# Mixers of a streaming-encoder layer: where the first weights, the state-space input and the projections' weights come from

## The chip, the cores and the metric

The kernel runs on one core of one Trainium2 chip. The metric is the device time of one execution in microseconds, the median of several. TensorE (PE) multiplies matrices, VectorE (DVE) and ScalarE (ACT) work on elements, GpSimd (POOL) gathers rows, and SyncE (SP) issues most transfers; ACT and POOL issue transfers too. Each engine runs its own instructions in order and waits on semaphores for the others.

## The reference

One layer over 1024 tokens of width 1024, float32: two token mixers in parallel on one input projection, then a retrieval of experts.

```python
xn = rms_norm(h, norm1_g)
p = xn @ w_in                                  # 1024 x 1536
xa, gate, us = p[..., :512], p[..., 512:1024], p[..., 1024:]
ya = rg_lru_group(xa, gate, ...)               # conv, gates, linear scan, times gelu(gate)
yb = s5_group(us, ...)                         # complex state-space scan, gelu, gated unit
y = concat([rms_norm(ya, gnorm_lru), rms_norm(yb, gnorm_s5)])
h = h + y @ w_out
h = h + peer_ffn(rms_norm(h, norm2_g), ...)    # 8 heads, top 16 of 128 x 128 experts
out = rms_norm(h, normf_g)
```

## The kernel before

**Precision.** Each large product is made of three: both operands are split into a high part (ACT copies it to the type fp32r) and a low part (DVE subtracts), and PE adds high x low, low x high and high x high. So every weight costs a transfer, an ACT copy and a DVE subtraction before PE can use it.

**Stages.** `front` (from L150) computes the mixers, up to the output projection and the second norm. `peer` (from L948) computes the queries, picks experts for all tokens, gathers rows for three blocks of 128 tokens (POOL fetches them, DVE consumes them) and treats the other five blocks densely: a first part that works ahead and stores its rows to DRAM (`aa` to `A_d`), and a steady part, `dense`, whose order is written out by hand.

**How the order comes about.** In `front` and in the first part of `peer` the pieces are Python generators. `Merge.run` keeps a planned clock for each engine, charges every instruction a planned cost, and lets the generator with the smallest clock plus bias emit next. A generator can wait for a flag by yielding its name. The framework then schedules the emitted instructions once more by its own cost model, with the emitted order as priority, so an instruction can be moved ahead of others that are not ready. Buffers are rings: a tile with `tag` and `bufs=n` waits until the tile n before it has been read for the last time.

**PSUM.** All eight banks are shared out in `front`: `pt` has four, `pj` two, `pu` two (L158 to L160).

**The first product, `us_first` (L258).** It computes columns 1024 to 1279 of the input projection, the first half of the state-space input, for eight groups of 128 tokens at once, in all eight banks (`held`), with a loop over eight slices k of the contraction. Each slice needs `split_x(k)` (L207) and a split slice of the weights (`wgroup`, L231). The weights `w0` come in one transfer of 1 MB from ACT's queue (L229), while SP's queue brings eight slices of x of 512 KB (L195). Beside it run `squares` (L213: the sums of squares of x, then `rc`, the reciprocal root per token, and its broadcast `rstdb` through PE, named spr) and `setup` (the state-space coefficients). When all slices are done, `us_first` waits for the flag "rc", and ACT copies each bank into `Vt` scaled by `rc` (`us_out`, L255).

**The rest of the input projection.** `proj(grp, ...)` (L604) computes 256 columns: it first has `wgroup` load and split eight weight slices of 128 x 256 (raw tiles `wr` with two buffers, split tiles `wh` and `wl` with nine), then makes four PSUM tiles, two halves e of 128 columns by two halves i of the tokens, 24 matmuls each, and DVE evacuates each with `rstdb`. `us_second` (L277) does columns 1280 to 1535. `proj_thread` (L685) runs proj 0, `us_second`, proj 1, and then proj 2 and 3 (the gates) after the flags "ut1" and "ut3", since their outputs take the place of `Vt`.

**Their consumers.** `quarter(q)` (L434) is the state-space scan for a quarter of the groups, mostly DVE; it starts its transposes of `Vt` (utp) after "us0" or "us1", and SP moves its matrix T in eight transfers (L479). `lru(m)` (L628) is the other mixer, for each 128 columns of proj 0 and 1. `glu` (L724, PSUM tiles glp) is the gated unit, `norm` (L784) gives the scales `rg`.

**Output projection, `w_out` (L813).** Sixteen PSUM tiles (`wop`) for each half, twelve matmuls each; DVE adds each to `h`, scaled by `rg` of that half. Both halves take `pj`, that is two banks.

Of the kernel before, what the change touches and what calls it, by code (L numbers as in the profile page):

```python
# [7 lines left out]
F32 = mybir.dt.float32  # L8
F32R = mybir.dt.float32r
# [3 lines left out]
AF = mybir.ActivationFunctionType  # L13
ALU = mybir.AluOpType
# [4 lines left out]
P = 128  # L19
D = 1024  # L20
T = 1024
L = 8
# [127 lines left out]
def front(tc, a, cst, nd, mg):  # L150


    nc = tc.nc
    V, S, G, PE = mg.V, mg.S, mg.G, mg.PE
# [3 lines left out]
    pt = lambda n: ps.tile([P, 512], F32, tag="mm", name=n, bufs=4)  # L158
    pj = lambda n: ps.tile([P, 512], F32, tag="pj", name=n, bufs=2)
    pu = lambda n: ps.tile([P, 512], F32, tag="us", name=n, bufs=2)  # L160
    keep = pools.open("fkeep")
    pxa = pools.open("fxa", "right")
    xa = [pxa.tile([P, 3 + T], F32, name=f"xa{m}") for m in range(4)]
# [3 lines left out]
    rstdb = keep.tile([P, T], F32, name="rstdb")  # L167
    rc = keep.tile([P, L], F32, name="rc")
# [5 lines left out]
    xh = pin.tile([P, 8, T], F32R, name="xh")  # L174
    xl = pin.tile([P, 8, T], F32R, name="xl")
# [7 lines left out]
    def t(shape, name):  # L183
        return pset.tile([P] + shape, F32, name=name)
# [5 lines left out]
    S.dma_start(Cin, a["s5c"])  # L190
    px = pools.open("fx")
    xrs = []
    for k in range(8):
        xr = px.tile([P, T], F32, name="xr", tag="xr", bufs=8)
        nc.sync.dma_start(xr, a["xT"][k * P:(k + 1) * P, :])  # L195
        xrs.append(xr)

    def spread(col):

# [7 lines left out]
    def split_x(k):  # L207
        S.activation(xh[:, k, :], xrs[k], AF.Copy, scale=g1[:, k:k + 1])
        V.scalar_tensor_tensor(xl[:, k, :], xrs[k], g1[:, k:k + 1], xh[:, k, :].bitcast(F32),
                               ALU.mult, ALU.subtract)  # L210
# [15 lines left out]
    pw = pools.open("fw", "right", bufs=9)  # L226
    pq = pools.open("fq", "right")
    w0 = pq.tile([P, 8, 256], F32, name="w0")
    nc.scalar.dma_start(w0, a["w_in"][:, 1024:1280].rearrange("(k p) n -> p k n", p=P))  # L229

    def wgroup(col, width, out, whole=None):  # L231

        for k in range(8):
            if whole is None:
                r = pw.tile([P, width], F32, tag="wr", name="wr", bufs=2)
                nc.sync.dma_start(r, a["w_in"][k * P:(k + 1) * P, col:col + width])
            else:
                r = whole[:, k]
            h = pw.tile([P, width], F32R, tag="wh", name="wh")
            lo = pw.tile([P, width], F32R, tag="wl", name="wl")  # L240
            S.activation(h, r, AF.Copy)
            V.tensor_tensor(lo, r, h.bitcast(F32), ALU.subtract)
            out.append((h, lo))
            yield


    Vt = {}

    def us_product(o, s, k, w):
        sl = slice(s * P, s * P + P)  # L250
        PE.matmul(o, xh[:, k, sl], w[k][1], start=(k == 0), stop=False)
        PE.matmul(o, xl[:, k, sl], w[k][0], start=False, stop=False)
        PE.matmul(o, xh[:, k, sl], w[k][0], start=False, stop=(k == 7))

    def us_out(hf, s, pp):  # L255
        S.activation(Vt[hf][:, :, s, :], pp.rearrange("p (g i) -> p g i", i=16), AF.Copy, scale=rc[:, s:s + 1])

    def us_first():  # L258

        w, held = [], [(pu if s < 2 else pj if s < 4 else pt)("usp")[:, :256] for s in range(L)]  # L260
        ws = wgroup(1024, 256, w, w0)
        for k in range(8):
            split_x(k)
            next(ws)
            yield
            for s in range(L):
                us_product(held[s], s, k, w)
            yield
        mg.flag("x")
        yield "rc"  # L270
        Vt[0] = pvt.tile([P, 16, L, 16], F32, name="Vt", tag="Vt", bufs=2)
        for s in reversed(range(L)):
            us_out(0, s, held[s])
            yield
        mg.flag("us0")

    def us_second():  # L277
        w = []
        yield from wgroup(1280, 256, w)
        Vt[1] = pvt.tile([P, 16, L, 16], F32, name="Vt", tag="Vt", bufs=2)  # L280
        for s in range(0, L, 2):
            pp = pu("usp")
            for e in range(2):
                o = pp[:, 256 * e:256 * e + 256]
                for k in range(8):
                    us_product(o, s + e, k, w)
                yield
                us_out(1, s + e, o)
                yield
        mg.flag("us1")  # L290


# [21 lines left out]
    def setup():  # L314
# [26 lines left out]
        f = t([16], "f")  # L341
# [56 lines left out]
        lo = 1  # L398
# [22 lines left out]
        yield  # L421
        V.tensor_tensor(f8l, f8, f8h, ALU.subtract)
        mg.flag("set")

    mg.run([(0.0, us_first()), (0.0, squares()), (2.0, setup())], until="x")
    pools.close("fx")
    p5 = pools.open("f5")
# [146 lines left out]
            yield  # L574
            S.activation(yB[:, q, 512 * h:512 * h + 512], pp, AF.Copy)

    mg.run([])
    pools.close("fq")

    pl = pools.open("fl", "right")  # L580
# [19 lines left out]
    sp4, spm8 = z2, sp  # L600
    V.tensor_scalar(sp4, sp, 4.0, None, ALU.mult)
    V.tensor_scalar(spm8, sp, -8.0, None, ALU.mult)

    def proj(grp, dst, by_s):  # L604

        w = []
        yield from wgroup(256 * grp, 256, w)
        for e in range(2):
            for i in range(2):
                sl = slice(512 * i, 512 * i + 512)  # L610
                pp = pj("pj")
                for k in range(8):
                    wh, wl = (x[:, e * P:(e + 1) * P] for x in w[k])
                    PE.matmul(pp, wh, xl[:, k, sl], start=(k == 0), stop=False)
                    PE.matmul(pp, wl, xh[:, k, sl], start=False, stop=False)
                    PE.matmul(pp, wh, xh[:, k, sl], start=False, stop=(k == 7))
                    if k % 4 == 3:
                        yield
                if by_s:
                    V.tensor_tensor(dst[e][:, sl], pp, rstdb[:, sl], ALU.mult)  # L620
                else:
                    sc = lambda x: x.rearrange("p (s c) -> p s c", c=P)
                    V.tensor_tensor(dst[e].rearrange("p (c s) -> p s c", s=L)[:, 4 * i:4 * i + 4], sc(pp),
                                    sc(rstdb[:, sl]), ALU.mult)
                yield
        mg.flag(f"proj{grp}")

    def lru(m):  # L628

# [53 lines left out]
        mg.flag("s5")  # L683

    def proj_thread():  # L685
        for grp in range(2):
            yield from proj(grp, [x[:, 3:] for x in xa[2 * grp:2 * grp + 2]], False)
            if grp == 0:
                yield from us_second()
        for grp in range(2):  # L690
            yield f"ut{2 * grp + 1}"
            y = pvt.tile([P, 2, T], F32, name="yA", tag="Vt", bufs=2)
            yA.extend([y[:, 0], y[:, 1]])
            yield from proj(2 + grp, yA[2 * grp:], True)
# [9 lines left out]
    def last():  # L704
# [8 lines left out]
        mg.flag("mixed")  # L713

    mg.run([(0.0, s5_thread()), (0.5, proj_thread()), (0.0, lru_thread(range(4))), (3.0, last())], until="s5")
    pools.close("f5", "fset")
    pg = pools.open("fg")
# [32 lines left out]
    def group_b():  # L750
        yield from glu()
        yield "wide"
        yield "norm0"
        yield from norm(1, [yB[:, k] for k in range(4)], gh, gl)
        yield from w_out(1)
# [53 lines left out]
    h = [(pacc if b < nd else phg).tile([P, D], F32, name=f"h{b}") for b in range(L)]  # L809
# [3 lines left out]
    def w_out(half):  # L813
        dh, dl = ((ah, al), (gh, gl))[half]
        yield f"norm{half}"
        yield f"wo{half}"
        todo = [(b, n) for b in reversed(range(L)) for n in range(2)]
        if half == 0:
            todo.sort(key=lambda x: x[1])
        for b, n in todo:  # L820
            bs = slice(b * P, b * P + P)
            ns = slice(512 * n, 512 * n + 512)
            pp = pj("wop")
            for k in range(4):
                wh, wl = wo[half][k, n]
                PE.matmul(pp, dh[:, k, bs], wl, start=(k == 0), stop=False)
                PE.matmul(pp, dl[:, k, bs], wh, start=False, stop=False)
                PE.matmul(pp, dh[:, k, bs], wh, start=False, stop=(k == 3))
            yield
            V.scalar_tensor_tensor(h[b][:, ns], pp, rg[half][:, b:b + 1], h[b][:, ns], ALU.mult, ALU.add)  # L830
            yield
            if half == 0 and (b, n) == (0, 0):
                mg.flag("cols0")
            if half and n:
                jk = po.tile([P, D], F32, name="jk", tag="sq2")
                S.activation(jk, h[b], AF.Square, accum_out=ss[:, b:b + 1])
                mg.flag(f"h{b}")
                yield
        mg.flag(f"half{half}")

    def group_a():
        yield from wo_half(0)
        yield from w_out(0)
# [871 lines left out]
```

## Time and profile before

| | us |
|---|---|
| median of 3 runs | 2697.93 |
| lowest, highest | 2694.83, 2700.26 |
| the profiled execution, time | 2685.19 |
| the profiled execution, span | 2683.4 |
| mixers up to the end of the first half of `w_out` | 0 to 347 |
| rest of `front` and first part of `peer` | 347 to 1552 |
| steady part and end | 1552 to 2683 |

The page gives busy time for each engine, the chain of work that ended last, and the costliest groups. Busy time is an average over stages with different limits, so the views that matter here are those by stretch of time, and the waits: who stood idle, and what ended the wait. The chain of the whole run goes through PE for 60% of the span and DVE for 21%.

### The profile page before, as it was taken

What the parts mean: (1) busy time and instruction counts of PE and PEld (TensorE: products, weight loads), DVE (VectorE), ACT (ScalarE), POOL (GpSimd) and SP (SyncE); (2) the same over time, 40 slices, a digit from 0 to 9 for tenths busy, and PEclk for the clock granted to TensorE, in tenths of its full rate; (3) what the DMA queues carried; (4) which work ended last, traced back from release to release, by engine and by line L of the source; (5) the groups of instructions that cost most, each with busy time, mean ns of one, the idle gap of its engine ahead of it and who ended that gap; (6) DMA issues with size and microseconds to landing.
All of it is one profiled execution on the core that took longest, in us unless ns stands there. A gap on an engine that the chain in (4) does not pass through costs nothing.

```text
span 2683.4 us, 40720 instructions
## 1 busy us (share of the span) xinstructions
PE 2517.4 (94%) x14623; PEld 2276.8 (85%) x14623; DVE 2364.5 (88%) x4541; ACT 1330.2 (50%) x2408; POOL 1172.7 (44%) x777
## 2 busy tenths in 40 slices
PE   5989899998999999999899889999899999999997
PEld 5766688998999999999899878888788888888885
DVE  6888649998999999999899779999888888999996
ACT  5457524322693965938739544444334333333432
POOL 0000000155573767847637535554444545555440
PEclk9989899999999999999999899999999999999998
DMA  5111324488899998999989989999899999999993
GB/s 169 32 35 37 126 80 127 147 281 313 275 401 317 354 392 306 396 341 357 401 276 364 388 321 331 332 328 323 291 329 326 330 324 329 333 329 327 329 330 133
DMA packets 298250, 755.39 MB, mean 282 GB/s; under 512 B 28352, under 2 KB 122752, under 8 KB 293312
## 3 DMA queue, kind: packets, MB, share of 16 engines
q0 software_dynamic: 110592, 402.70, 41.6%
q1 hardware_dynamic: 180720, 338.90, 35.6%
q10 hardware_dynamic: 6736, 11.19, 1.2%
q8 instruction: 115, 1.88, 0.3%
q14 instruction: 87, 0.71, 0.1%
HBM read 665.54 MB, written 85.98 MB: 280 GB/s over the span
## 4 chain that ended last, share of the span: by engine, by line
PE 60%; DVE 21%; DMA 9%; ACT 6%; issue 4%; ACTq 0%; SPq 0%; POOL 0%; DVEq 0%; POOLq 0%
PE vp L146 25%; PE ap L146 17%; PE total L146 6%; DMA A_d<-aa 4%; PE qp L146 4%; ACT ohB L146 3%; PE gp L146 3%; PE wop L146 3%; DVE row L146 2%; DVE oh L146 2%; DVE ul L146 2%; PE pj L146 2%; DVE hb L146 1%; DVE ix L146 1%; DMA nf<-in_gf_dram 1%
## 5 line engine op out<-in xcount | busy, mean ns | idle before, releaser
L1233 POOL DMA_INDIRECT row<-in_peer_u_dram,idx x384 | 562.6, 1465 | 961.0 <-DVE scv L146 495.6
L1233 POOL DMA_INDIRECT row<-in_peer_v_dram,idx x384 | 607.3, 1581 | 448.0 <-DVE hb L146 328.8
L146 PE MATMUL ap<-xDl,uh 128*128 128x320 f32 x2048 | 655.4, 320 | 30.5 <-ACT aa L146 23.9
L146 PE MATMUL ap<-xDh,ul 128*128 128x320 f32 x2048 | 648.0, 316 | 8.5 <-DVE ul L146 8.5
L146 PE MATMUL ap<-xDh,uh 128*128 128x320 f32 x2048 | 645.8, 315 | 0.0
L146 DVE SCALAR_TENSOR_TENSOR hb<-row,act,hb 128x1024 f32<-128x1024 f32 x384 | 492.3, 1282 | 8.9 <-DMA row<-in_peer_v_dram,idx 4.5
L146 DVE CUSTOM_DVE_ANT_0 row<-row,xg 128x1024 f32<-128x1024 f32 x384 | 458.4, 1219 | 15.4 <-DMA row<-in_peer_u_dram,idx 7.8
L146 PEld LDWEIGHTS ap<-xDl,uh 128*128 128x128 f32 x2048 | 392.5, 192 | 34.7 <-ACT aa L146 26.5
L146 PE MATMUL vp<-vl,hh 128*128 128x512 f32 x1024 | 400.7, 391 | 12.4 <-DVE vl L146 10.8
L146 PEld LDWEIGHTS ap<-xDh,ul 128*128 128x128 f32 x2048 | 392.3, 192 | 12.2 <-DVE ul L146 10.6
L146 PE MATMUL vp<-vh,hl 128*128 128x512 f32 x1024 | 399.9, 391 | 0.0
L146 PE MATMUL vp<-vh,hh 128*128 128x512 f32 x1024 | 399.6, 390 | 0.0
L146 PEld LDWEIGHTS ap<-xDh,uh 128*128 128x128 f32 x2048 | 391.7, 191 | 0.0
L146 ACT ACTIVATE gq<-gt 128x640 f32<-128x640 f32 x128 | 175.1, 1368 | 330.9 <-DVE hr L146 325.2
L146 DVE TENSOR_TENSOR ul<-ur,uh 128x1024 fp32r<-128x1024 f32 x128 | 155.9, 1218 | 97.3 <-ACT uh L146 97.2
L146 PEld LDWEIGHTS vp<-vl,hh 128*128 128x128 f32 x1024 | 193.0, 189 | 53.4 <-DVE vl L146 11.6
L146 PEld LDWEIGHTS vp<-vh,hh 128*128 128x128 f32 x1024 | 193.1, 189 | 40.5
L146 PEld LDWEIGHTS vp<-vh,hl 128*128 128x128 f32 x1024 | 193.2, 189 | 38.8
L146 PE MATMUL gp<-ohB,ohA 128*128 128x128 f32 x1280 | 198.1, 281 | 18.8 <-ACT gs L146 12.0
L146 ACT ACTIVATE aa<-ap 128x320 f32<-128x320 f32 x194 | 84.5, 437 | 258.8 <-PE ap L146 207.0
L146 ACT ACTIVATE ohB<-ohB,kt 128x128 f32<-128x128 f32 x480 | 204.4, 497 | 0.0
L146 PEld LDWEIGHTS gp<-ohB,ohA 128*128 128x128 f32 x1280 | 179.7, 193 | 24.4 <-ACT gs L146 13.3
(440 smaller groups left out, 4498.3 us busy)
## 6 DMA issues: line engine op xcount, KB each, us to landing
ur<-in_uT_dram SPq DMA_DIRECT2D x128, 512.0 KB, 6.7
vr<-in_peer_v_dram SPq DMA_DIRECT2D x128, 512.0 KB, 6.2
gt<-G_d SPq DMA_DIRECT2D x32, 1280.0 KB, 9.7
G_d<-gs SPq DMA_DIRECT2D x19, 2048.0 KB, 25.6
A_d<-aa SPq DMA_DIRECT2D x96, 320.0 KB, 8.6
hr<-A_d SPq DMA_DIRECT2D x96, 320.0 KB, 5.9
wqr<-in_wq_dram SPq DMA_DIRECT2D x31, 512.0 KB, 3.9
row<-in_peer_u_dram,idx POOLq DMA_INDIRECT x384, 7.2
```

Source lines behind the costliest of these rows:

```text
L146: return fn(*args, **kw)
L1233: G.indirect_dma_start(out=r, out_offset=None, in_=a["peer_v" if at >= P else "peer_u"], in_offset=bass.IndirectOffsetOnAxis(ap=idx[n][:, ...
```

## The change

The first weights come in eight slices of 128 KB, each issued on SP's queue right behind its slice of x. The eight banks of `us_first` are copied to `Vt` unscaled, without waiting for `rc`; a flag "held" is set; when "rc" is there, DVE multiplies the eight parts of `Vt` by it. The projections take their weights in steps of 128 columns: a tile of 128 x 256 now holds two slices of 128 columns, loaded by two transfers of 64 KB. All weight tiles stand in one list (`wseq`), in the order proj 0, second state-space half, proj 1, 2, 3. `wtake(n)` makes sure that the next n exist, and `wfill` makes more, up to nine (`WBUFS`) ahead of what has been used. `proj` takes four tiles, fills up, and then makes the two PSUM tiles of that step. Proj 0 starts after "held", in the run in which `squares` and `setup` end; its evacuations wait for "rc". The first half of `w_out` takes its PSUM tiles from `pt` (four banks), the second from `pj` as before.

```diff
-    for k in range(8):
-        xr = px.tile([P, T], F32, name="xr", tag="xr", bufs=8)
-        nc.sync.dma_start(xr, a["xT"][k * P:(k + 1) * P, :])
-        xrs.append(xr)
...
     w0 = pq.tile([P, 8, 256], F32, name="w0")
-    nc.scalar.dma_start(w0, a["w_in"][:, 1024:1280].rearrange("(k p) n -> p k n", p=P))
-
-    def wgroup(col, width, out, whole=None):
...
+    for k in range(8):
+        xr = px.tile([P, T], F32, name="xr", tag="xr", bufs=8)
+        nc.sync.dma_start(xr, a["xT"][k * P:(k + 1) * P, :])
+        xrs.append(xr)
+        nc.sync.dma_start(w0[:, k], a["w_in"][k * P:(k + 1) * P, 1024:1280])
+
+    WBUFS = 9
+    wseq, wmade, wused = [], [], [0]
+    for n in range(8):
+        wseq.append([w0[:, n]])
+    for part in (0, 1, None, 2, 3, 4, 5, 6, 7):
+        for n in range(8 if part is None else 4):
+            if part is None:
+                wseq.append([a["w_in"][n * P:(n + 1) * P, 1280:1536]])
             else:
+                wseq.append([a["w_in"][(2 * n + i) * P:(2 * n + i + 1) * P, P * part:P * part + P] for i in range(2)])
+
+    def wnext():
+
+        parts = wseq[len(wmade)]
+        if len(wmade) < 8:
+            r = parts[0]
+        else:
+            r = pw.tile([P, 256], F32, tag="wr", name="wr", bufs=2)
+            w = 256 // len(parts)
+            for i, x in enumerate(parts):
+                nc.sync.dma_start(r[:, w * i:w * i + w], x)
+        h = pw.tile([P, 256], F32R, tag="wh", name="wh")
+        lo = pw.tile([P, 256], F32R, tag="wl", name="wl")
+        S.activation(h, r, AF.Copy)
+        V.tensor_tensor(lo, r, h.bitcast(F32), ALU.subtract)
+        wmade.append((h, lo))
+
+    def wfill(end=8 + 9 * 4 + 4):
+        while len(wmade) < min(wused[0] + WBUFS, len(wseq), end):
+            wnext()
+            yield
+
+    def wtake(n):
+        yield from wfill(wused[0] + n)
+        return wmade[wused[0]:wused[0] + n]
...
             for s in range(L):
-                us_product(held[s], s, k, w)
+                us_product(held[s], s, k, wmade)
             yield
+        wused[0] = 8
         mg.flag("x")
-        yield "rc"
         Vt[0] = pvt.tile([P, 16, L, 16], F32, name="Vt", tag="Vt", bufs=2)
         for s in reversed(range(L)):
-            us_out(0, s, held[s])
+            S.activation(Vt[0][:, :, s, :], held[s].rearrange("p (g i) -> p g i", i=16), AF.Copy)
             yield
+        mg.flag("held")
+        yield "rc"
+        for s in range(L):
+            V.tensor_scalar(Vt[0][:, :, s, :], Vt[0][:, :, s, :], rc[:, s:s + 1], None, ALU.mult)
         mg.flag("us0")

     def us_second():
-        w = []
-        yield from wgroup(1280, 256, w)
+        w = yield from wtake(8)
...
+        wused[0] += 8
         mg.flag("us1")
...
+    def proj(grp, dst, by_s):
+
+        for e in range(2):
+            w = yield from wtake(4)
+            yield from wfill()
+            for i in range(2):
+                sl = slice(512 * i, 512 * i + 512)
+                pp = pj("pj")
+                for k in range(8):
+                    wh, wl = (x[:, k % 2 * P:k % 2 * P + P] for x in w[k // 2])
...
+                if i:
+                    wused[0] += 4
+                if grp == 0:
+                    yield "rc"
...
+    def proj_first():
+        yield "held"
+        yield from proj(0, [x[:, 3:] for x in xa[:2]], False)
...
-    mg.run([])
+    mg.run([(0.5, proj_first())], until="us0")
     pools.close("fq")
...
     def proj_thread():
-        for grp in range(2):
-            yield from proj(grp, [x[:, 3:] for x in xa[2 * grp:2 * grp + 2]], False)
-            if grp == 0:
-                yield from us_second()
+        yield "proj0"
+        yield from us_second()
+        yield from proj(1, [x[:, 3:] for x in xa[2:]], False)
...
-            pp = pj("wop")
+            pp = (pj if half else pt)("wop")
```

More of the change, by code (lines that the diff above doesn't have):

```diff
@@ L228, in front @@
     w0 = pq.tile([P, 8, 256], F32, name="w0")
-    nc.scalar.dma_start(w0, a["w_in"][:, 1024:1280].rearrange("(k p) n -> p k n", p=P))
-    def wgroup(col, width, out, whole=None):
[L233 to L236, printed above, removed]
-            else:
[L238 to L243, printed above, removed]
+    for k in range(8):
[11 more added lines that the diff above has]
+                wseq.append([a["w_in"][n * P:(n + 1) * P, 1280:1536]])
+            else:
+                wseq.append([a["w_in"][(2 * n + i) * P:(2 * n + i + 1) * P, P * part:P * part + P] for i in range(2)])
[16 more added lines that the diff above has]
+            wnext()
             yield
+    def wtake(n):
+        yield from wfill(wused[0] + n)
+        return wmade[wused[0]:wused[0] + n]
     Vt = {}
@@ L258, in us_first @@
     def us_first():
-        w, held = [], [(pu if s < 2 else pj if s < 4 else pt)("usp")[:, :256] for s in range(L)]
-        ws = wgroup(1024, 256, w, w0)
+        held = [(pu if s < 2 else pj if s < 4 else pt)("usp")[:, :256] for s in range(L)]
         for k in range(8):
             split_x(k)
-            next(ws)
+            wnext()
             yield
             for s in range(L):
-                us_product(held[s], s, k, w)
+                us_product(held[s], s, k, wmade)
             yield
+        wused[0] = 8
         mg.flag("x")
-        yield "rc"
         Vt[0] = pvt.tile([P, 16, L, 16], F32, name="Vt", tag="Vt", bufs=2)
         for s in reversed(range(L)):
-            us_out(0, s, held[s])
+            S.activation(Vt[0][:, :, s, :], held[s].rearrange("p (g i) -> p g i", i=16), AF.Copy)
             yield
+        mg.flag("held")
+        yield "rc"
+        for s in range(L):
+            V.tensor_scalar(Vt[0][:, :, s, :], Vt[0][:, :, s, :], rc[:, s:s + 1], None, ALU.mult)
         mg.flag("us0")
     def us_second():
-        w = []
-        yield from wgroup(1280, 256, w)
+        w = yield from wtake(8)
         Vt[1] = pvt.tile([P, 16, L, 16], F32, name="Vt", tag="Vt", bufs=2)
@@ L423, in setup @@
         mg.flag("set")
+    def proj(grp, dst, by_s):
[7 more added lines that the diff above has]
+                    wh, wl = (x[:, k % 2 * P:k % 2 * P + P] for x in w[k // 2])
+                    PE.matmul(pp, wh, xl[:, k, sl], start=(k == 0), stop=False)
+                    PE.matmul(pp, wl, xh[:, k, sl], start=False, stop=False)
+                    PE.matmul(pp, wh, xh[:, k, sl], start=False, stop=(k == 7))
+                    if k % 4 == 3:
+                        yield
[3 more added lines that the diff above has]
+                    yield "rc"
+                if by_s:
+                    V.tensor_tensor(dst[e][:, sl], pp, rstdb[:, sl], ALU.mult)
+                else:
+                    sc = lambda x: x.rearrange("p (s c) -> p s c", c=P)
+                    V.tensor_tensor(dst[e].rearrange("p (c s) -> p s c", s=L)[:, 4 * i:4 * i + 4], sc(pp),
+                                    sc(rstdb[:, sl]), ALU.mult)
+                yield
+        mg.flag(f"proj{grp}")
+    def proj_first():
+        yield "held"
+        yield from proj(0, [x[:, 3:] for x in xa[:2]], False)
     mg.run([(0.0, us_first()), (0.0, squares()), (2.0, setup())], until="x")
@@ L602, in front @@
     V.tensor_scalar(spm8, sp, -8.0, None, ALU.mult)
[L604 to L626, printed above, removed]
     def lru(m):
```

## The prediction

> **What bounds the kernel now.** I read the page first, then busy time by stretches, then what TensorE (PE) and VectorE (DVE) waited for in the first 310 us, then the order of instructions at each long wait, and last the chain that ended last in the second half.
>
> ```profile
> span 2683.4 us, 40720 instructions
> ```
> ```profile
> 0.00:46.00 46.00, 26.01 (x192) 24.96 (x192) 29.49 (x118) 24.87 (x55) 2.81 (x9) 1.00 0.65 224
> 46.00:80.00 34.00, 26.05 (x161) 21.26 (x162) 25.17 (x71) 15.86 (x34) 0.00 (x0) 0.85 0.17 45
> 80.00:170.00 90.00, 75.11 (x549) 58.35 (x547) 84.29 (x129) 53.29 (x77) 0.00 (x0) 0.96 0.12 30
> 170.00:230.00 60.00, 54.17 (x325) 41.46 (x326) 46.46 (x73) 29.34 (x40) 0.00 (x0) 0.95 0.12 32
> 230.00:307.00 77.00, 65.51 (x273) 49.40 (x274) 57.76 (x69) 55.44 (x71) 0.00 (x0) 0.95 0.32 113
> 380.00:1152.00 772.00, 739.41 (x4986) 722.56 (x4985) 732.01 (x2050) 435.61 (x1019) 398.96 (x248) 0.98 0.83 295
> 1152.00:1552.00 400.00, 357.04 (x2449) 350.69 (x2447) 357.07 (x881) 245.32 (x587) 227.67 (x154) 0.95 0.97 355
> 1552.00:2640.00 1088.00, 1076.88 (x5273) 929.40 (x5273) 969.69 (x1046) 440.42 (x481) 543.26 (x367) 0.99 0.90 321
> ```
>
> The columns of the second view: stretch and its length, then busy us (and instructions) of PE, its weight loads, DVE, ACT and POOL, then PE's granted clock, DMA's share, GB/s. The change lies in the mixers, 0 to 347 us. From 380 us on PE is busy 96%, 89% and 99% of three stretches: work there follows work, and nothing waits for a fixed point in time, so what the mixers gain should move everything behind them. In the mixers no engine is full. DVE is the fullest, with 64 us idle of 307 (0 to 46: 16.5; to 80: 8.8; to 170: 5.7; to 230: 13.5; to 307: 19.2). PE and DVE feed each other, so I count the gain mainly in DVE idle time that goes, and not in PE waits and DVE waits added together.
>
> ```profile
> PE usp L146 <- DVE wl L146: 17.9, 4, 15.6
> PE wtp L146 <- issue: 9.1, 1, 9.1
> PE pj L146 <- DVE wl L146: 8.7, 3, 7.4
> PE wop L146 <- DVE h L146: 5.5, 1, 5.5
> ```
> ```profile
> DVE Wr L146 <- PE inr L146: 13.3, 3, 7.8
> ...
> DVE yA L146 <- PE pj L146: 3.5, 2, 2.7
> ```
> ```profile
> DVE wl L146 <- ACT wh L146: 8.0, 2, 5.7
> ```
>
> These are the waits (total, times, longest; the last row is that of 0 to 46 us alone). Each of the four PE rows belongs to one part of the change: the first weights, the state-space input held in PSUM, the weights of the projections, the output projection's PSUM.
>
> **A, first weights by slices (0 to 46 us).**
>
> ```profile
> 4.93 1.28 ACT L146 ACT_TABLE_LOAD   x1 [4.93 <-DMA xr<-in_xT_dram]
> 6.23 1.15 ACT L146 ACTIVATE xh<-xr,g 128x1024 fp32r<-128x1024 f32 x1
> 14.67 0.42 ACT L146 ACTIVATE wh<-w 128x256 fp32r<-128x256 f32 x1 [7.29 <-DMA w<-in_w_in_dram]
> ...
> 15.60 0.58 PE L146 MATMUL usp<-wl,xh 128*128 128x256 f32 x1 [15.60 <-DVE wl L146]
> ```
> ```profile
> 10.00:20.00 10.00, 4.40 (x23) 1.00 1.01 385
> ```
> ```profile
> 15.04 0.91 SPq L236 DMA_DIRECT2D wr<-in_w_in_dram  x2
> ```
>
> The first slice of x is there at 4.93, the megabyte of weights not before 14.67; ACT stands 7.29 in between. With a 128 KB slice behind each 512 KB slice of x on the same SP queue, at 385 GB/s (the row of 10 to 20 us, DMA share 1.01) a slice of weights costs 0.33 us. So xh ends at 7.4, wh at 7.8, wl at 8.2: the first product starts 7.4 earlier. The rest follows: eight pairs, 5.24 MB, take 13.6 us at that rate. The last pair then lands about 18, 27 us before the last product ends (44.9, below). DVE's 16.5 idle us of this stretch hold 8.0 in which it waited for wh; that is the room. The queues: ACT loses one issue, SP gets eight of 0.45 (last row; 3.6 us, beside 14 us of transfers). The x rows for the squares, 16 x 256 KB issued from ACT's queue, stood behind the wait that goes; they can now start earlier and contend, and this is the lower bound's reason. **I take -7**, bounds -8 and 0 (x delayed as much as the weights come earlier).
>
> **B, the input copied unscaled (46 to 80 us).**
>
> ```profile
> 44.58 0.28 PE L146 MATMUL usp<-wh,xh 128*128 128x256 f32 x1
> ...
> 53.39 3.01 ACT L146 ACTIVATE Vt<-usp,rc 128x256 f32<-128x256 f32 x8
> 53.95 1.94 PE L146 MATMUL wtp<-ident,WB 128*128 128x128 f32 x8 [9.09 <-issue]
> ...
> 61.99 0.50 PE L146 MATMUL pj<-xl,wh 128*128 128x512 f32 x1
> ```
> ```profile
> 50.00:60.00 10.00, 6.05 (x26) 0.50 0.18 53
> ```
>
> The eight products hold all eight PSUM banks. They end at 44.9, but their copies scale by rc and so start at 53.39; PE has no bank for 9.09 us ("issue" is the bank), comes back at half clock (0.50), and the first projection starts at 61.99. After the change the copies follow the last product. About 3 us later two banks are free and the projection starts: with A at about 41, some 20 earlier than now. That is PE time, and DVE does not get all of it: from 46 to 80 DVE was idle 8.8 us. New on DVE are eight multiplications by rc.
>
> ```profile
> L146 DVE TENSOR_TENSOR wl<-wr,wh 128x256 fp32r<-128x256 f32 x40 | 16.3, 419 | 1.4 <-ACT wh L146 1.4
> ...
> L146 DVE TENSOR_SCALAR ph<-ph 128x512 f32<-128x512 f32 x4 | 1.7, 426 | 4.5 <-ACT Es L146 4.5
> ```
>
> One is 128x256. The first row has that size but two tensor sources (0.42); the second is the same operation at twice the size (0.43), so half of it, 0.21, is the lower end: 1.7 to 3.4 for eight. I take 0.3, nearer to the same operation: 2.4. They stand ahead of quarter 0's transposes, with other DVE work of quarter 0 beside them. The copies on ACT keep their count and form. The new wait: the projection's evacuations wait for the broadcast of rc (the squares), and behind them PE's third projection group, with two banks. The squares have room to come early: ACT was idle 21 of the first 46 us. **I take -8.8 + 2.4 + 1.0** (a wait for ACT's sine stays; the second row has 4.5 for four) **= -5.4**, bounds -8.8 and +3.4.
>
> **C, D, E, weights 128 columns, one step ahead.**
>
> ```profile
> ACT wh L146 <- DMA wr<-in_w_in_dram: 27.2, 9, 10.2
> ```
> ```profile
> wr<-in_w_in_dram SPq DMA_DIRECT2D x40, 128.0 KB, 2.1
> ```
> ```profile
> 172.65 0.80 PE L146 MATMUL pj<-xh,wl 128*128 128x512 f32 x1 [7.41 <-DVE wl L146]
> ```
>
> Now eight slices are split before a group's products, through two raw buffers and 2.1 us per transfer; ACT stood 27.2 us for them. Then four tiles suffice and the next four are made while PE works. Splits keep their count and form (40 of 0.42 on each engine). Issues of the eight projection steps double: 64 for 32, 32 x 0.45 = 14.4 us of SP spread over 200 us. On SP, the moves of T (L479) stand behind a weight issue that waits for its raw buffer. Behind a split that waits for PE to free its slot stands all of ACT.
>
> From 80 to 170 DVE is 94% busy: **C, 0**. From 170 to 230 it is idle 13.5, 7.8 of it behind inr. The 7.41 of PE at 172.65 is a late split of the second group; the change prefetches only one tile of it while the other half of the state-space input is computed, so three more must still be split at that point, not seven. **D: half, -6.5**, bounds -13.5 and 0. From 230 on, the 3.5 us of yA behind pj go if PE keeps its lead: **E: -3**, bounds -8 and 0.
>
> **F, four PSUM buffers for the first half of the output projection.**
>
> ```profile
> 306.19 0.69 ACT L146 ACTIVATE sg<-glp,cols 128x512 f32<-128x512 f32 x1
> ```
> ```profile
> 306.76 0.79 PE L146 MATMUL wop<-wol,ah 128*128 128x512 f32 x1 [5.54 <-DVE h L146]
> ...
> 312.04 0.63 PE L146 MATMUL wop<-wol,ah 128*128 128x512 f32 x1
> 312.47 0.57 PE L146 MATMUL wop<-woh,al 128*128 128x512 f32 x1
> 312.88 0.39 PE L146 MATMUL wop<-woh,ah 128*128 128x512 f32 x1
> 313.11 0.40 PE L146 MATMUL wop<-wol,ah 128*128 128x512 f32 x1
> ```
>
> Two tiles are full, the norm's scale is late, PE stands 5.54 and then runs at half clock until 312.6: 0.43 from start to start, 0.23 after. Two more tiles are 24 products x 0.23 = 5.5 us, just the wait; the half clock from 306.76 to 312.6 cost half of 5.85, 2.9. The four banks are shared with the gated unit, whose last tile is read at 306.19, so three may be there: one tile more, -2.7. **I take -5**, bounds -8.4 and 0.
>
> [...]
>
> **Sum:** -7 - 5.4 + 0 - 6.5 - 3 - 5 = -26.9, say **-27**. The profiled execution took 2685.19 (span 2683.4): 2658 by it. The median shown is 2697.93, 12.7 above that execution; the gain is absolute time in a stage, so I take it off the median: **2671**.
>
> **Rivals.**
> 1. *The parts do not add up.* DVE, 94% busy from 80 to 170, takes A and F and gives back the rest in other waits (the 7.8 behind inr is in no part's name): -7 - 5 = -12, **2686**. For it: C to E have the widest bounds. Against it: PE is 20 us ahead.
> 2. *Slower, through the stores of the second stage.* Three buffers hold the rows that go to A_d; PE's next product waits when the store of the oldest is late.
>
> ```profile
> 1434.90 28.27 DMA A_d<-aa
> ...
> 1487.37 38.59 DMA A_d<-aa
> ```
> These rows are of the chain that ended last (start, length). DMA is 97% busy there, and PE idle 43 of 400 us. The order of that work comes from planned clocks which the new front end shifts. It decides if one more store of the 38.59 kind meets a full DMA: -27 + 38.6 = +11.6, **2709.5**. For it: the chain passes through three such waits after 1152 us. Against it: nothing in that code changes.
> 3. *The same, the other way:* one 28.27 wait fewer, **2643**.
> 4. *The slices do not come earlier*, since SP's queue puts them behind all of x: A falls away, **2678**.
>
> **How the numbers follow.** Forecast 0.53 (its own range 2656 to 2684), rival 1 0.23, rival 2 0.10, rival 3 0.09, rival 4 0.05. The range reaches from 2645 to 2700: the forecast, rivals 1 and 4 with their bounds (the repeats before lie between 2694.83 and 2700.26), without rival 2 and most of rival 3. 0.2%, what a measurement of this kernel can tell from no change, is 5.4 us. Faster is all of the forecast, 3 and 4, and 0.17 of rival 1: 0.84. Same 0.06, slower 0.10.
>
> **What would show it.** A: the first usp product at about 8 us, the last at about 38. B: Vt copies right behind it, the first pj product near 41, no 9 us wait, PEclk near 1.0 from 50 to 60, eight multiplications of 0.2 to 0.4. C to E: ACT's wait for wr well under 27, PE's wait at the second group under 4. F: no 5.5 wait of wop for h, clock 1.0 behind it. Whole: the output projection starts about 22 us earlier, and the steady stage (from 1552) about 27. The forecast is wrong if DVE's idle time up to the output projection hardly falls below 64, or if the stretch from 380 to 1552 gets longer.

## The result, and the profile after

| | before | after | ratio, 95% interval |
|---|---|---|---|
| first comparison, median us | 2696.38 | 2665.51 | 0.9891 [0.9864, 0.9919] |
| second comparison (below), median us | 2688.13 | 2668.96 | 0.9921 [0.9886, 0.9956] |
| profiled execution, span us | 2683.4 | 2656.0 | |

The change makes the kernel faster by 31 and 19 us in two comparisons. The sum of the prediction said 27. What follows shows that this sum came out near for the wrong reason: its terms do not add. One execution each of undo B and steps (4473 us) and of the kernel before beside only steps (4070 us) ran at a lower granted clock (0.77 and 0.56) and is left out of the medians below.

The mixers by stretches, cut at the same four events in both kernels: end of the first products, first xa evacuation, last xa evacuation, first addition to h in `w_out`. ("xa" is what DVE makes of a tile of proj 0 or 1 when it evacuates it.) Columns as in the prediction: length, then busy us of PE, weight loads, DVE, ACT and POOL. First before, then after:

```profile
0.00:44.60 44.60, 25.74 (x192) 24.90 (x192) 28.12 (x116) 23.60 (x50) 2.81 (x9) 1.00 0.67 231
44.60:68.10 23.50, 14.41 (x85) 11.42 (x84) 18.82 (x63) 15.58 (x34) 0.00 (x0) 0.78 0.18 49
68.10:195.90 127.80, 110.26 (x758) 86.87 (x758) 113.64 (x173) 62.00 (x93) 0.00 (x0) 0.95 0.12 31
195.90:306.00 110.10, 96.19 (x472) 71.99 (x466) 81.59 (x106) 76.64 (x95) 0.00 (x0) 0.97 0.26 87
```
```profile
0.00:41.00 41.00, 26.40 (x191) 26.00 (x192) 28.29 (x117) 22.29 (x49) 2.73 (x9) 0.96 0.65 223
41.00:62.20 21.20, 16.60 (x109) 13.35 (x108) 16.29 (x41) 12.80 (x33) 0.00 (x0) 1.00 0.40 119
62.20:164.10 101.90, 96.13 (x670) 76.88 (x670) 94.69 (x170) 57.47 (x89) 0.00 (x0) 0.98 0.15 36
164.10:275.20 111.10, 97.87 (x498) 73.68 (x497) 99.20 (x137) 73.80 (x96) 0.00 (x0) 0.94 0.28 88
```

Length less DVE's busy time is DVE's idle time: before 16.5, 4.7, 14.2 and 28.5 (63.8 of 306), after 12.7, 4.9, 7.2 and 11.9 (36.7 of 275.2). DVE's work itself is nearly the same, 242.2 and 238.5 us. So the first addition to h comes 30.8 earlier, 27 of them idle time of DVE. Most of it goes in the *last* stretch, far behind the first products and the first projection (experiment 3 shows that it goes there even when nothing in that stretch is changed): work of DVE that stood at the end of the projections (113.64 to 94.69) now fills what was idle there.

The waits that the prediction named, in the first 310 us of after (total, times, longest):

```profile
PE usp L146 <- DVE wl L146: 18.0, 4, 10.5
ACT wh L146 <- DMA wr<-in_w_in_dram: 16.4, 10, 5.8
...
PE wop L146 <- issue: 4.3, 1, 4.3
...
DVE Wr L146 <- PE inr L146: 2.8, 1, 2.8
...
PE spr L146 <- DVE rc L146: 2.2, 1, 2.2
...
DVE yA L146 <- PE pj L146: 0.6, 1, 0.6
```

Gone are PE's 9.1 at wtp, its 8.7 for the low parts of projection weights (2.4 for a high part has come) and its 5.5 for h. ACT's wait for raw weights falls from 27.2 to 16.4, and the 7.8 behind inr is gone too. The first row has hardly moved (17.9 before): the wait for the first weights is now spread over the slices.

How far the gain travels: the first query products start at 397.9 before and 373.4 after (-24.5). A fixed point behind them is the first selection of experts on stored scores, before and after:

```profile
646.87 0.49 DVE L146 MAX8 v<-s 128x8 f32<-128x128 f32 x2 [1.56 <-DMA s<-S_d]
```
```profile
619.82 0.49 DVE L146 MAX8 v<-s 128x8 f32<-128x128 f32 x2 [3.83 <-DMA s<-S_d]
```

That is -27.1; the steady part starts 26.7 earlier and the span ends 27.4 earlier. From the first query on, every engine has the same instructions in the same order in both kernels.

### The profile page after: what moved, and what is told of

Same layout as the page of the kernel before. It is cut to its first block, busy times and chain, and to the rows that moved or that the text cites. A ratio compares the mean times of both kernels' runs of the same rounds, so it can differ in the third digit from the quotient of the medians.

```text
span 2656.0 us, 40788 instructions
## 1 busy us (share of the span) xinstructions
PE 2508.6 (94%) x14623; PEld 2272.5 (86%) x14623; DVE 2363.7 (89%) x4549; ACT 1322.6 (50%) x2404; POOL 1157.8 (44%) x777
## 4 chain that ended last, share of the span: by engine, by line
PE 59%; DVE 23%; DMA 9%; ACT 5%; issue 3%; SPq 0%; ACTq 0%; DVEq 0%
PE vp L146 25%; PE ap L146 16%; PE total L146 6%; DMA A_d<-aa 4%; PE qp L146 3%; PE gp L146 3%; ACT ohB L146 3%; PE wop L146 3%; DVE oh L146 2%; DVE row L146 2%; DVE ul L146 2%; DMA ur<-in_uT_dram 1%; DVE hb L146 1%; DVE ix L146 1%; DVE ci L146 1%
## 5 line engine op out<-in xcount | busy, mean ns | idle before, releaser
L1263 POOL DMA_INDIRECT row<-in_peer_v_dram,idx x384 | 594.2, 1547 | 456.9 <-DVE hb L146 332.3
L146 PE MATMUL ap<-xDh,ul 128*128 128x320 f32 x2048 | 646.9, 316 | 9.0 <-DVE ul L146 8.9
L146 PE MATMUL gp<-ohB,ohA 128*128 128x128 f32 x1280 | 198.1, 281 | 24.5 <-ACT gs L146 16.9
```

Of the source, the lines that this page charges most:

```text
L146: return fn(*args, **kw)
L1263: G.indirect_dma_start(out=r, out_offset=None, in_=a["peer_v" if at >= P else "peer_u"], in_offset=bass.IndirectOffsetOnAxis(ap=idx[n][:, ...
```

## The experiments

Two sets. "Undo" kernels are the changed kernel with one part put back; "only" kernels are the kernel before with one part added. The ratio is to the kernel before. The last three columns are the times in us of the first addition to h, of the first query product and of the first selection.

| kernel | ratio [95%] | DVE idle up to first h | first h | queries | selection |
|---|---|---|---|---|---|
| before | | 63.8 | 306.0 | 397.9 | 646.9 |
| after | 0.9891 [0.9864, 0.9919] | 36.7 | 275.2 | 373.4 | 619.8 |
| undo A: weights in one transfer | 0.9930 [0.9891, 0.9969] | 36.4 | 274.7 | 372.7 | 622.0 |
| undo B: scaled copies | 0.9884 [0.9845, 0.9924] | 43.8 | 281.6 | 371.0 | 621.6 |
| undo steps | 0.9881 [0.9826, 0.9936] | 36.3 | 276.4 | 364.9 | 622.7 |
| undo early projection | 0.9878 [0.9829, 0.9927] | 39.4 | 280.8 | 366.5 | 624.5 |
| undo F: two banks | 0.9897 [0.9856, 0.9938] | 34.4 | 272.1 | 362.4 | 621.2 |
| undo B and steps | 0.9958 [0.9930, 0.9985] | 58.7 | 299.0 | 384.8 | 632.6 |
| only B | 0.9882 [0.9830, 0.9935] | 44.5 | 285.0 | 375.6 | 623.6 |
| only steps | 0.9908 [0.9882, 0.9934] | 44.5 | 283.2 | 374.2 | 621.6 |
| only F | 0.9974 [0.9951, 0.9997] | 66.2 | 307.2 | 393.9 | 640.7 |

**1. One part put back at a time.**

```diff
 undo A
-        nc.sync.dma_start(w0[:, k], a["w_in"][k * P:(k + 1) * P, 1024:1280])
+    nc.scalar.dma_start(w0, a["w_in"][:, 1024:1280].rearrange("(k p) n -> p k n", p=P))
 undo B
+        yield "rc"
...
         for s in reversed(range(L)):
-            S.activation(Vt[0][:, :, s, :], held[s].rearrange("p (g i) -> p g i", i=16), AF.Copy)
+            us_out(0, s, held[s])
...
-        yield "rc"
-        for s in range(L):
-            V.tensor_scalar(Vt[0][:, :, s, :], Vt[0][:, :, s, :], rc[:, s:s + 1], None, ALU.mult)
 undo steps
...
+        w = yield from wtake(8)
         for e in range(2):
-            w = yield from wtake(4)
-            yield from wfill()
...
 undo F
-            pp = (pj if half else pt)("wop")
+            pp = pj("wop")
```

> The changed kernel with the first weights again in one transfer of 1 MB from ACT's queue; the rest as changed. Theory (the parts add up, A is worth about 7): first product at about 15.6 us instead of 10.5, first evacuation of the output projection about 5 to 7 us later than 275.2, time about 5 to 7 us above the changed kernel's 2665.5. Rival (the new gate is rc, whose squares compete with x for the transfers; a later first product costs nothing): first product late, but the broadcast of rc near 60 us or earlier and the first evacuation of the output projection within 2 us of 275.2.

> The changed kernel with the state-space input again copied by ACT scaled by rc, after rc is there; no multiplications on DVE. Theory (parts add up, B is worth about 5): first projection product near 57 instead of 41.2, first evacuation of the output projection about 5 us later than 275.2, time about 5 us above 2665.5. Rival (the 20 us of lead of PE in the projections is what later fills DVE's idle time from 170 to 230, so B carries most of the gain): first evacuation 15 to 25 us later, time 15 to 25 above. Second rival (DVE is the bound, and rc gates the first projection's evacuations in either form): under 2 us.

> The changed kernel with the projections' weights again in groups of 256 columns, eight tiles split before each group and nothing made ahead. Theory (D and E, 9.5 together): first evacuation of the output projection about 9 us later than 275.2, DVE idle again about 7 us between 160 and 222, time about 9 above 2665.5. Rival (the lead comes from the early start of the projections alone): within 3 us.

> The changed kernel with both halves of the output projection in two PSUM buffers. Theory as predicted (F is worth 5): a PE wait of 5 us for the norm's scale comes back and the queries start 3 to 8 us later than 373.4. Rival (PE has the gated unit's products, 60 of which the changed kernel computes inside this stage, to fill the wait): the queries start within 1 us of 373.4, time the same as the changed kernel's.

All four stay faster than before, with intervals that overlap that of the whole change. These intervals reach 10 to 15 us to each side, so in the time a loss of 5 to 7 us would not show; the times of the first h tell more. Undo B loses 6.4 there, about what the sum gave B (5.4), but nothing of it is left at the queries (371.0). The steps, given 9.5, lose 1.2 at the first h, A and F nothing. Without F the queries even start 11 us earlier, and the time is no better. Two questions were open after this: which part carries the gain, and why an earlier query start brings nothing.

**2. What all four had kept.** All of them still emit the first projection early (`proj_first`, beside squares and setup). It was put back to its old place:

```diff
-    mg.run([(0.5, proj_first())], until="us0")
+    mg.run([])
...
-        yield "proj0"
+        yield from proj(0, [x[:, 3:] for x in xa[:2]], False)
         yield from us_second()
```

> The changed kernel with one thing put back: the first projection step is emitted again where it was (first in the thread of the projections, after the input's first half, with nothing of it running in the stretch that ends the squares and the setup). Slices, unscaled copies, 128-column steps and four output banks stay. None of the four kernels that put back one of those lost the gain, and all four kept this early projection. Theory 'the early projection is the carrier': the first pj product comes after 55 us, the last xa evacuation after 185, the first h evacuation after 292, and the time is 2680 to 2690. Theory 'the parts replace each other' (any of the early starts fills the same DVE idle time, 63.8 us of the first 306 before and 36.7 of 275 after): first h evacuation 274 to 283, DVE idle ahead of it under 45, time 2664 to 2673.

Measured: first pj product 49.3, last xa evacuation 180.4, first h 280.8, 0.9878. It isn't the carrier.

**3. Two parts put back together, and one alone.** The two edits of undo B and undo steps in one kernel; and the kernel before with the unscaled copies and the early projection only, or with the steps and the early projection only.

> Two parts put back together: the state-space input is copied scaled after rc again, and the projections take 256 columns with nothing made ahead of a group. What stays: slices of the first weights, the first projection emitted early, four output banks. Each of the two alone put back left the first h evacuation at 281.6 and 276.4 (changed kernel 275.2, before 306.0). Theory 'the parts replace each other': with both gone the gain goes too: the projections again take some 125 us from the first to the last xa evacuation (127.8 before, 102 to 110 with either part), first h evacuation 295 to 303, DVE idle ahead of it over 55, time 2680 to 2692. Theory 'neither carries the gain': first h evacuation under 285, time 2664 to 2675.

> The kernel before with one part of the change: the input is copied unscaled as soon as the products end, and the first projection is emitted early behind it. First weights in one transfer, 256-column groups with nothing made ahead, two banks for the output projection, as before. Theory 'the parts replace each other': this part alone gives nearly all of what the mixers gain, first pj product near 44, last xa evacuation 168 to 176, first h evacuation 276 to 283, time 2664 to 2676. The sum of the prediction gives this part -5.4: first h evacuation about 300, time 2688 to 2696.

> The kernel before with one part of the change: the projections in steps of 128 columns, with the next step's weights split ahead and the first projection in the stretch of squares and setup. First weights in one transfer, copies scaled after rc, two banks for the output projection, as before. The unscaled copies alone gave 0.9882, all but these two parts 0.9958. Theory 'either of the two fills the same idle time of DVE': last xa evacuation 176 to 186 (195.9 before), first h evacuation 284 to 292, time 2664 to 2676. Theory 'the steps only help on top of an early start': last xa evacuation over 188, first h evacuation over 295, time 2680 to 2695. The sum of the prediction gives these steps -9.5.

The last stretch (last xa evacuation to first h) of undo B and steps, of only B, and of only steps:

```profile
187.60:299.00 111.40, 101.18 (x482) 75.58 (x476) 80.33 (x105) 75.55 (x94) 0.00 (x0) 0.95 0.26 86
```
```profile
180.60:285.00 104.40, 96.47 (x518) 74.51 (x516) 90.27 (x126) 75.48 (x98) 0.00 (x0) 0.99 0.28 93
```
```profile
179.90:283.20 103.30, 94.52 (x488) 72.91 (x486) 88.42 (x119) 76.58 (x99) 0.00 (x0) 0.99 0.29 92
```

With both gone, DVE is idle 31.1 in that stretch again, and all that is left of the gain is some 0.4% (2679.79 against 2692.08, -12.3). With either alone it is idle 14.1 or 14.9 there, and the time is -25.9 (2666.23 against 2692.08) or -22.7 (2666.72 against 2689.43). So **B and the steps do the same thing**: with either, PE runs ahead of DVE in the projections, and either lead is enough to fill DVE's idle time later on. DVE's waits show it: up to the first h, those that PE ended add up to 23.1 us before and 20.6 with both put back, but to 8.9 in only B, 9.2 in only steps and 6.1 in the changed kernel. The edits also shift the planned order of the mixers' instructions; what the shifted order does by itself was not tested. B, with the early projection, brings alone what the whole change brings; the expectation for "the parts replace each other" gave the time of all three kernels and the first h within 2 us of its bounds; the last xa evacuation of only B came later than it said (180.6, for 168 to 176).

**4. F alone.**

> The kernel before with one part of the change: the first half of the output projection takes its tiles from the four banks. The sum of the prediction gives it -5 (0 to -8.4): the 5.5 us wait for h and the half clock behind it go, queries start 5 us earlier (393 instead of 397.9), time 2689 to 2696. The kernel with this part alone put back started its queries 11 us EARLIER than the changed one, because more of the gated unit's second half runs inside the projection when four banks are there. Theory 'F costs at the queries': queries start at 397 to 405, time 2695 to 2703 or no change.

Queries at 393.9 (-4.0), time 2687.98 against 2692.08 (-4.1, with an interval that only just leaves out no change): the sum's -5 held on the kernel before; "F costs at the queries" fell there. In the changed kernel it does cost. There `w_out` starts while the gated unit is at work, whose tiles (glp) take the same four banks. From 246 to 270, with F (the changed kernel) and without (undo F):

```profile
246.00:270.00 24.00, 17.29 (x55) 12.16 (x54) 17.98 (x19) 15.22 (x20) 0.00 (x0) 0.79 0.63 223
```
```profile
246.00:270.00 24.00, 20.17 (x92) 15.71 (x93) 17.76 (x22) 17.42 (x23) 0.00 (x0) 1.00 0.53 196
```

PE makes 55 products instead of 92 (31 of the gated unit instead of 52), and at clock 0.79 instead of 1.00. From the first h to the queries it is then busy without a break in both (95.96 of 98.2 us and 89.86 of 90.3), so 37 products x 0.23 = 8.5 us of work made later are an estimated 8.5 of the 11 us. The half clock (0.50 from 256.3 to 266.4 us) came behind a pause of PE that both kernels have. ACT issues the loads of `h` from its own queue, and stands for 7.12 us ahead of the high part `ah` (`al`, `wol` and the first product of `w_out` come behind it), here in the changed kernel:

```profile
244.40 7.81 ACTq L841 DMA_DIRECT2D h<-in_x_dram  x6
252.25 1.15 ACT L146 ACTIVATE ah<-yA,cols 128x1024 fp32r<-128x1024 f32 x1 [7.12 <-issue]
```

In undo F the wait is 7.12 as well, but PE has 12 more products of the gated unit to make in it: it pauses 1.59 us and the clock stays at 1.00, where the changed kernel pauses 4.32.

**5. Why earlier queries bring nothing.** In the table the selection follows the queries by 246 to 251 us in all kernels whose queries start at 371 or later, and by 258 to 259 in the three that start earlier: it never comes before about 620 (618.0 in experiment 6). ACT in undo F, with the selection behind it on DVE:

```profile
585.53 0.44 ACT L146 ACTIVATE qt<-qp 128x320 f32<-128x320 f32 x1 [3.08 <-PE qp L146]
603.94 0.44 ACT L146 ACTIVATE qt<-qp 128x320 f32<-128x320 f32 x1 [17.97 <-remote]
611.09 0.44 ACT L146 ACTIVATE qt<-qp 128x320 f32<-128x320 f32 x1 [6.72 <-remote]
```
```profile
621.22 0.49 DVE L146 MAX8 v<-s 128x8 f32<-128x128 f32 x2 [15.79 <-DMA s<-S_d]
```

The products that these evacuations read had ended by 592.5 ("remote": an event ended the wait whose cause the profile does not know). Meanwhile POOL gathers rows at a DMA share of 1.03 (590 to 600). Does it go if fewer rows are in flight?

```diff
-ROWS = 8
+ROWS = 6
```

> Two banks for the output projection again (the queries then start earliest, 362.4 us), and the ring of gathered rows cut from 8 tiles to 6 (the planned order of the second stage shifts with it). In nine profiled kernels the first selection of experts from stored scores (the first MAX8 on a loaded s) starts 247 to 251 us after the queries as long as these start after 370 us, but never before about 620: with queries at 362 to 367 us it came at 621 to 624, and ACT stood up to 18 us ahead of an evacuation whose product had ended, while gathers kept the DMA share at 1.02 to 1.03. Theory 'gathered rows in flight hold the scores back': with fewer in flight ACT's standing in 585 to 616 us falls below 8 us, the selection starts at 610 to 616, and the time is 2650 to 2662. Theory 'the hold has another origin': ACT still stands over 15 us there, the selection stays at 620 to 625, time 2664 to 2680. Either way a smaller ring can cost DVE waits for rows later on.

> As the one before with 4 tiles in the ring. Theory 'gathered rows in flight hold the scores back': DMA share under 0.95 in 590 to 610 us, no standing of ACT over 4 us there, selection at 609 to 614. Three rows in flight may be too few for the gathers themselves: DVE's waits for rows, 4 us in 570 to 690 now, grow, and the whole is slower than with 8, over 2680. Theory 'another origin': selection at 620 or later, with ACT standing as with 8.

The stretch from 585 to 616 with 8 rows, the same with 6, and the selection with 6:

```profile
585.00:616.00 31.00, 14.13 (x79) 13.35 (x78) 18.49 (x30) 3.02 (x8) 17.30 (x18) 0.67 0.95 378
```
```profile
585.00:616.00 31.00, 26.25 (x163) 25.78 (x162) 23.44 (x65) 6.66 (x13) 19.07 (x16) 0.89 1.02 404
```
```profile
611.08 0.48 DVE L146 MAX8 v<-s 128x8 f32<-128x128 f32 x2
```

With 6 the two holds are gone, PE works 26.25 of 31 us instead of 14.13, and the selection follows the queries (364.4) by 246.6 again: the selection came where the first theory put it. This does not show that the rows in flight are the cause, though. The smaller ring also changes the planned order, and that from about 405 us on, ahead of the holds: at 405.7 ACT splits `uh` in undo F, and with 6 rows it evacuates `qt` in that place of its order. The time did not come where the theory put it: it is 2673.51 (0.9932 [0.9893, 0.9970]), no better, and from the selection to the steady part it takes 947 us instead of 921 to 934. With 4 rows the two holds are gone too and the DMA share from 590 to 610 is 0.96 for 1.03, but the selection comes at 615.8, 254.3 behind the queries, where 609 to 614 was expected. The time is 2817.83 (1.0471 [1.0435, 1.0507]): DVE waits for rows, where undo F has 3.9 us of the first row below in the whole run and none of the second:

```profile
DVE row L146 <- DMA row<-in_peer_u_dram,idx: 124.9, 104, 4.4
DVE hb L146 <- DMA row<-in_peer_v_dram,idx: 89.4, 85, 4.0
```

What exactly ACT waited for stays open: the DMA share was 1.02 with 6 rows too, where nothing was held.

**6. The changed kernel once more.**

> The changed kernel once more, with its own profile. Its first profile was the fastest of its four runs (2657.8 of 2657.8 to 2671.24), and its stretch from the first query to the steady part took 1167 us, where the four kernels with one part put back took 1180 to 1191 for the same instructions in the same order. If that difference is the run and not the kernel, this profile has the same times up to the queries (first h evacuation 274 to 277, queries 372 to 375) and 1175 to 1190 us behind them, and the median is 2662 to 2670. If it is the kernel: 1165 to 1170 again, and a median under 2662.

First query to steady part, first profile and second:

```profile
373.40:1540.80 1167.40, 1089.24 (x7448) 1069.90 (x7447) 1095.65 (x2936) 685.92 (x1608) 615.25 (x402) 0.97 0.89 320
```
```profile
371.50:1551.90 1180.40, 1092.41 (x7449) 1073.92 (x7448) 1094.75 (x2935) 686.41 (x1608) 627.56 (x402) 0.97 0.88 316
```

The same program, the same busy times of PE, DVE and ACT within 0.3%, 13 us apart, all behind the selection (619.8 and 618.0). The execution of the first profile (2657.8) was the shortest of four. So differences of some 13 us behind the queries, undo kernels included, are not to be explained by a kernel's edits; up to the queries the two profiles agree within 4 us. The first h (272.4) and the queries (371.5) came up to 1.6 us ahead of what was expected here, so differences of 1 to 3 us in those columns of the table mean nothing.

## Why the prediction was right, and where it was not

The time (2671, range 2645 to 2700) and the sign held. The 0.2% that the prediction took as the least that can be told from no change was small: the intervals here reach 0.2 to 0.6% to each side. Point by point:

- **"I count the gain mainly in DVE idle time that goes."** Right, and the best step of it: 27.1 of the 30.8 us at the first h are DVE idle time. The warning sign, that this time would hardly fall below 64, did not appear (36.7).
- **A, -7.** The mechanism was right, the size off. The evacuation chain starts as follows in after:

```profile
10.47 0.58 PE L146 MATMUL usp<-wl,xh 128*128 128x256 f32 x1 [10.47 <-DVE wl L146]
10.54 0.63 ACT L146 ACTIVATE xq<-xq 128x512 f32<-128x512 f32 x1 [2.49 <-DMA xq<-in_x_dram]
...
17.07 0.63 ACT L146 ACTIVATE xq<-xq 128x512 f32<-128x512 f32 x1 [4.37 <-DMA xq<-in_x_dram]
```

The first product came at 10.5 (8 foreseen), 5.1 earlier, but the last one only 3.6 earlier (38 foreseen, 41.0). ACT now waited for rows of the squares between two slices, the reason given for the lower bound. Put back alone, A leaves the first h where it is (274.7 for 275.2); its time, 0.9930, isn't told apart from that of the whole change. Beside B it adds nothing that could be seen.
- **B, -5.4.** The steps came as foreseen, and so did what was late next:

```profile
38.84 0.74 ACT L146 ACTIVATE Vt<-usp 128x256 f32<-128x256 f32 x2 [6.52 <-PE usp L146]
...
41.16 0.40 PE L146 MATMUL pj<-xl,wh 128*128 128x512 f32 x1
...
60.05 2.19 DVE L146 TENSOR_SCALAR Vt<-Vt,rc 128x256 f32<-128x256 f32 x8
...
62.16 1.10 DVE L146 TENSOR_TENSOR xa<-pj,rstdb 128x512 f32<-128x512 f32 x1
```

Projection at 41.2 (41 foreseen), eight multiplications in 2.19 us (2.4). The copies, in order on ACT, kept the squares behind them for 6.5, so rc came at 60 and the first evacuation only 5.9 earlier. In their own windows, then, A and B together are worth 5.9, where the sum had 12.4; in only B, without A, that evacuation comes 3.7 earlier (64.4). **The step that failed** is the one that made this its whole price: "That is PE time, and DVE does not get all of it: from 46 to 80 DVE was idle 8.8 us." Twenty us of lead on PE do not expire at 80 us. B alone gave -25.9, and 14.4 of its 19.3 us of DVE idle time went after the last xa evacuation.
- **C, D, E, 0 - 6.5 - 3.** The signs were there: ACT's wait for weights 16.4 (27.2), DVE's waits behind inr and pj 2.8 and 0.6 (13.3 and 3.5). D's idle time went whole: DVE was busy 59.71 of 60 us from 162 to 222, where half was taken. (The 7.8 behind inr are within D's 13.5, so rival 1 is wrong to call them in no part's name.) But the steps alone gave -22.7, for the same reason as B.
- **F, -5.** -4.1 on the kernel before. In the changed kernel the wait for h is gone, but the sign "clock 1.0 behind it" failed, and 6 of the 30.8 us of lead at the first h are given back before the queries: the forecast counted the banks that `w_out` wins, not those that the gated unit loses to it (experiment 4).
- **The sum.** B (-25.9), the steps (-22.7) and what is left without both (-12.3) would be -61 if they added; the change brings -31 and -19. (The early projection is in all three, but experiment 2 shows that it isn't the carrier.) The prediction gave each part the idle time of its own window. That counted no idle time twice and kept the total near, but it made the term of B too small by a factor of about five and those of the steps by more than two: the idle time of DVE is one stock that several parts draw on. That the total fits so well is in part luck. The first product of the output projection came 29.4 earlier (255.4 for 284.8), where the sum without F had 22; from there to the queries 5 us were lost again, where the sum had F gain 5.
- **"What the mixers gain should move everything behind them."** True of the first profile (-24.5, -27.1, -26.7, -27.4), with a limit that the busy shares did not show: a lead at the queries beyond about 371 us stops at the selection. In the second profile the same four points come 26.5, 28.8, 15.7 and 16.6 earlier: part of the lead is within what one profile and the next differ by.
- **Rivals.** Rival 1 named the right worry, parts that don't add, but the wrong survivors: A and F with the early projection are what is left (-12.3, its 12) when B and the steps go. Rivals 2 and 3 rested on a shifted order of the second stage; that order did not shift. The chain passes two long waits for A_d after 1152 us (28.99 and 25.25) instead of three, and yet the time from the selection to the steady part stayed the same (920.6 and 921.0); what made up for it is not shown, and the second profile took 933.9 there. Rival 4 fell: the first slices came 5.1 earlier.

## What to carry to other kernels

Where one engine works through a fixed load and idles in several places, its idle time is one stock: price a part by how long its lead can last downstream, not by the idle time of the window in which it is made, and ask of every two parts whether they draw on the same stock. Then try each part alone on the old kernel: here the unscaled copies with the early projection do alone what the whole change does, which putting parts back one at a time could not show. And look for the first point behind the change where an earlier arrival is no longer passed on.

## What the runs showed of the hardware

The half clock lasted some 10 us in the changed kernel, and 3.8 us of unbroken work in it did not end it. PE in after, at the start of `w_out` (start and length; in brackets the idle time ahead):

```profile
255.42 0.47 PE L146 MATMUL wop<-wol,ah 128*128 128x512 f32 x1 [4.32 <-issue]
...
257.80 0.80 PE L146 MATMUL wop<-woh,al 128*128 128x512 f32 x1 [0.52 <-DVE al L146]
...
260.95 0.63 PE L146 MATMUL wop<-woh,ah 128*128 128x512 f32 x1
262.61 1.22 PE L146 MATMUL wop<-wol,ah 128*128 128x512 f32 x2 [1.03 <-ACT ah L146]
...
266.19 0.53 PE L146 MATMUL wop<-woh,al 128*128 128x512 f32 x1
266.56 0.39 PE L146 MATMUL wop<-woh,ah 128*128 128x512 f32 x1
```

After the pause of 4.32 three products took 0.40 to 0.47 us each (granted clock 0.96 from 255.4 to 256.3 us), the next two 0.80, and those behind them 0.63 up to 266.2 us. The granted clock was 0.50 from 256.3 to 266.4 us, 0.99 from 250 to 256.3 and 1.00 from 266.4 to the first h at 275.2. From 257.80 to 261.58 PE worked without a pause, 3.8 us, and the clock did not come back; a pause of 1.03 followed, and then 3.6 to 3.9 us of unbroken work, from 262.61, behind which the products took 0.39 again. In the kernel before, the half clock behind the pause of 5.54 us lasted 5.85 us (the prediction's rows for F), with PE busy throughout. What sets these lengths is not shown.

A multiplication of 128x256 in place by a value for each row took 0.348 us (0.26 from start to start, eight in 2.19), where half of the 128x512 row (0.426) would be 0.21: the smaller operation is not half as long here. Its elements also lie apart in `Vt`; whether that adds to its time was not measured.
